# Pacing the first two tiles of an out-projection, and the queue order of one load and one cast

## The chip, the cores and the metric

The kernel runs on one NeuronCore of a Trainium2 chip. A core has engines that run side by side and meet only at semaphores: TensorE (PE) multiplies matrices, VectorE (DVE) and ScalarE (ACT) work element by element, GpSimd (POOL) does so more slowly, and SyncE (SP) mostly issues DMA transfers. Matmul results land in PSUM, eight banks per partition, from which DVE and ACT fetch them. The metric is the device time of one execution in microseconds (us), lower is better.

## What is computed

One layer of a hybrid decoder for 1024 positions of width 1024. After an RMS norm, one input projection gives the parts for eight heads of differential attention and four heads of gated linear attention (GLA). The attention part, which the change touches, is for each head

```python
s = einsum('bqhmd,bkhmd->bhmqk', qb, k)            # two maps m per head, q scaled
p = softmax(where(mask, s, -inf), axis=-1)         # causal
w = p[:, :, 0] - lam * p[:, :, 1]
o = einsum('bhqk,bhkv->bqhv', w, v)
...
oa = rms_norm(o, subln_g) * (1 - lam_init) * silu(ga)
y = einsum('bse,ed->bsd', concatenate([oa, ob], -1), w_out)   # out-projection, ob from GLA
out = x + rms_norm(y, post_g)
```

## The kernel before

**Precision and tiles.** Factors are split into a high and a low part (a rounding cast on ACT, then the remainder by a subtraction on DVE), and a product is three matmuls, high by high and the two mixed ones. The positions are eight tiles of 128; a matmul has up to 512 columns.

**Phase 1** (to about 624 us) projects the input and runs the GLA heads. It stores q, k, the values and the GLA output ("mix") to DRAM scratch, and at its end loads the first halves of the out-projection's weights (`wo_hi`, `wo_lo`, slices 8 to 15) and the first tile's mix (`mix0`).

**Phase 2** (to about 920 us) interleaves three streams of PE work, each a generator that yields the cost of what it just traced:

- `all_scores` (line 1223): for each head and each block of 128 queries, from the last (7) down to the first, and for both maps, the scores `sc` (two matmuls for each part of up to 512 keys, in one of three PSUM banks used in turn). DVE masks and reduces them to a minimum (`p<-sc,maskt`), ACT takes the exponential (`p<-p,stt`), POOL scales the second map's probabilities, and DVE subtracts them (`p<-p,stt,p`).
- `all_values` (line 1311): `turn` (1243) transposes these probabilities on PE (`wtr`), casts the high part on ACT (`wt_hi`, line 1253) and subtracts the low part on DVE (`wt_lo`). `weigh` (1257) multiplies them by the values (`po`), two turns behind. After the last one of a half, ACT copies the result to `o`, and `attn_norm` (1271) takes its norm: two squares on ACT (`fold`, line 1283, and `sq`), a sum on DVE, its high and low part (`sq_hl`), a matmul with ones (`ms`), and what follows from it (`r`, `gate`).
- `out_early` (line 1415): the out-projection of the GLA half (`ypart`), tile by tile in two PSUM banks, one for each half of the columns. In tile 0 a step is one slice for both halves, six matmuls, with a yield of 1.0 before and after it; in tiles 1 to 6 a step is three matmuls with a yield of 0.69. A finished bank is copied by ACT (`yst`) and stored. Later this stream does the attention half for heads that are done, and at the end, in `mix_pair` (1499), casts the last heads' mix (`m_hi<-m_raw`) and puts earlier sums into banks (`yps<-yp`) for the last products.

`merge` (line 1106) decides the order: each stream has a clock that runs from a begin to an end, a yield of cost c moves it by c times (end - begin) / total cost, and the stream whose clock is least traces next. The scores have 288 units of time for a cost of 8 x 20.3, from 0. The values begin at 32. `out_early` begins at -6 and ends at 342 with a total cost of 149.24, a number that is written out by hand. PE keeps the order so made (`keep_in_program_order` in `mm` and `tr`); so do the few DMAs marked in the same way. On ACT, DVE and POOL, and for the other DMAs of SP, the compiler sets the order, and each of these queues then runs in that order.

**What the change touches.** `mix(1)` (line 1422) loads the second tile's mix, two transfers of 512 KB issued by SP and kept in order; it is now called in the first step of `out_early`, after `v_first = load_v(0)` (line 1151) has issued head 0's values. `turn` writes the cast of `wt_hi` at line 1253; `attn_norm` its first square at 1283; `mix_pair` its cast at 1504.

After phase 2, `finish` (1592) ends the tiles one after the other: the last products, the norm of each row, and the output.

Of the kernel before, what the change touches and what calls it, by code (L numbers as in the profile page):

```python
# [10 lines left out]
AF = mybir.ActivationFunctionType  # L11
# [9 lines left out]
DA_HEADS = 8  # L21
# [10 lines left out]
def hymba_kernel(  # L32
# [42 lines left out]
    act, dve, pool = Queue(nc.scalar), Queue(nc.vector), Queue(nc.gpsimd)  # L75

    def fp(t):
        return t.bitcast(F32)

    def cols(half):  # L80
        return slice(half * 512, half * 512 + 512)
# [47 lines left out]
    def bank(i, shape, name):  # L129
        return psum.tile(shape, F32, tag=f"b{i}", name=name)  # L130
# [10 lines left out]
    def mm(*a, **k):  # L141
        tc.keep_in_program_order(pe.matmul(*a, **k))  # L142

    def tr(dst, src):
        tc.keep_in_program_order(pe.transpose(dst, src, ident))  # L145
# [114 lines left out]
    i = order.index((1, 4))  # L260
# [792 lines left out]
    E, wo = D // P, {}  # L1053
# [18 lines left out]
    def mix_tiles():  # L1072
        n_mix[0] += 1
        return [
            hw.tile([P, 8, P], F32R, tag=f"s2_{n}{n_mix[0] % 2}", name=f"m_{n}")
            for n in ("hi", "lo")
        ]

    def mix(st):

        part = mix_tiles()
        for t in range(2):
            ins = sp.dma_start(fp(part[t]), mixe[st, t])
            if st < 2:
                tc.keep_in_program_order(ins)
        return part
# [54 lines left out]
    def load_v(h):  # L1141
        v = [smp.tile([P, NT, P], F32R, tag="v", name=f"v{t}", bufs=4) for t in range(2)]
        for t in range(2):

            with tc.issue_after(qk_load[0]) if h else nullcontext():
                ins = sp.dma_start(fp(v[t]), v_d[h // 4][h % 4, t])
            if h == 0:
                tc.keep_in_program_order(ins)
        return v

    v_first = load_v(0)

    n_sc, n_tr = [0], [0]
# [5 lines left out]
    def tr_bank(name, shape):  # L1159
        n_tr[0] += 1  # L1160
        return bank(TR[n_tr[0] % 2], shape, name)
# [77 lines left out]
    def blocks_of(kt, half):  # L1239

        return range(max(kt - 4 * half, 0), 4)

    def turn(h, half, kts):

        pt = tr_bank("wtr", [P, 512])
        n = 0
        for kt in kts:
            for i in blocks_of(kt, half):
                tr(pt[:, n : n + P], w[h, 4 * half + i][:, kt * P : (kt + 1) * P])
                n += P  # L1250
        hi = smp.tile([P, 512], F32R, tag="wt_hi", name="wt_hi", bufs=3)
        lo = smp.tile([P, 512], F32R, tag="wt_lo", name="wt_lo", bufs=3)
        act.copy(hi[:, :n], pt[:, :n])
        dve.tensor_tensor(lo[:, :n], pt[:, :n], fp(hi[:, :n]), ALU.subtract)
        return hi, lo

# [14 lines left out]
    def attn_norm(h, half, o):  # L1271
        if h < DA_HEADS - 1:
            gate = smp.tile([P, 512], F32, tag="gate", name="gate", bufs=2)
        else:
            gate = kp.tile([P, 512], F32, tag=("q1", "k1")[half], name="gate")
        with tc.issue_after(qk_load[0]):
            sp.dma_start(gate, g_d[h][:, cols(half)])
        sq = smp.tile([P, 512], F32, tag="r", name="sq", bufs=1)


        hl = smp.tile([P, 512], F32R, tag="sq_hl", name="sq_hl", bufs=1)
        fold = smp.tile([P, 512], F32, tag="fold", name="fold", bufs=1)
        act.activation(fold[:64], o[64:], AF.Square)
        act.activation(sq[:64], o[:64], AF.Square)
        dve.tensor_tensor(sq[:64], sq[:64], fold[:64], ALU.add)
        act.copy(hl[:64], sq[:64])
        dve.tensor_tensor(hl[64:], sq[:64], fp(hl[:64]), ALU.subtract)
        if h == DA_HEADS - 1:

            dve.scalar_tensor_tensor(gate, o, sub_g, gate, ALU.mult, ALU.mult)  # L1290
        for _ in range(4):
            yield 0.0
        n_tr[0] += 1
        ms = bank(TR[n_tr[0] % 2], [P, 512], "ms")
        mm(ms, ones, hl, start=True, stop=True)
        if h == DA_HEADS - 1 and not half:
            opened[TR[n_tr[0] % 2]] = None
        r = smp.tile([P, 512], F32, tag="r", name="r", bufs=1)
        act.activation(r, ms, AF.Ln, bias=eps_t, scale=1.0 / P)
        act.activation(r, r, AF.Exp, scale=-0.5)  # L1300
        if h < DA_HEADS - 1:
            dve.scalar_tensor_tensor(r, o, sub_g, r, ALU.mult, ALU.mult)
            pool.tensor_tensor(gate, r, gate, ALU.mult)
            sp.dma_start(mixd[h * P : (h + 1) * P, cols(half)], gate)
            stored.append(h)
        else:
            dve.tensor_tensor(gate, gate, r, ALU.mult)
            last_mix[half] = gate
        yield 0.0
# [97 lines left out]
    def y_bank(st, dh, name):  # L1407
        return bank(Y[dh], [P, 512], name)
# [6 lines left out]
    def out_early():  # L1415

        part = mix0
        ps = [y_bank(0, dh, "ypart") for dh in range(2)]
        for e in range(E, E + 8):
            yield 1.0  # L1420
            if e == E:
                nxt = mix(1)
            for dh in range(2):
                times(ps[dh], part, E, dh, e, E + 7)
            yield 1.0
        for dh in range(2):
            sp.dma_start(yd[0][dh], y_tile(ps[dh]))
        for st in range(1, NT - 1):
            part, nxt = nxt, mix(st + 1)
            rows = slice(ENDS[st - 1] * P, ENDS[st - 1] * P + P)  # L1430
            sp.dma_start(out[0, rows, :], x[0, rows, :])
            for dh in range(2):
                ps = y_bank(st, dh, "ypart")
                for e in range(E, E + 8):
                    times(ps, part, E, dh, e, E + 7)
                    yield 0.69
                sp.dma_start(yd[st][dh], y_tile(ps))

        yield lambda: len(stored) >= 7
        part = nxt  # L1440
        ps = [y_bank(NT - 1, dh, "ypart") for dh in range(2)]
        raws_o = [load_mix(st, 0, 4) for st in ENDS[:3]]
        for e in range(E, E + 8):
            for dh in range(2):
                times(ps[dh], part, E, dh, e, E + 7)
                yield 0.69
            if e < E + 4:
                weights(e - E)
            if e == E + 6:
                nxt = mix_part(ENDS[0], 0, 4, raws_o.pop(0))  # L1450
        for dh in range(2):
            kept = sp.dma_start(yd[NT - 1][dh], y_tile(ps[dh]))
        for n, st in enumerate(ENDS):
            part = nxt
            if n == 1:
                yield lambda: len(stored) >= 8
            if n + 3 < NT:
                raws_o.append(load_mix(ENDS[n + 3], 0, 4))

            if 1 <= n <= 4:  # L1460
                with tc.issue_after(kept.ins), tc.issue_after(mix_load[0]):
                    weights(3 + n)
            if n + 1 < NT:
                nxt = mix_part(ENDS[n + 1], 0, 4, raws_o.pop(0))
            for dh in range(2):
                ps = y_bank(st, dh, "ypart")
                for e in range(4):
                    times(ps, part, 0, dh, e, 3)
                    yield 0.69
                pool.dma_start(yd[st][dh], y_tile(ps), accum_op=ALU.add)  # L1470
        yield lambda: len(stored) >= 2 * (DA_HEADS - 1) - 1
        mix_pair(0)
        for n, st in enumerate(ENDS[:2]):
            if n:
                yield lambda: scored
            for dh in range(2):
                seed(st, dh, (Y, SC)[n][dh], sums_of(n)[:, dh])
            yield 0.7
        for st in ENDS[:2]:
            for dh in range(2):  # L1480
                for e in range(4, 7):
                    last_times(st, dh, parts_d[st], e)
                    yield 0.69
            if st == ENDS[0]:
                mix_pair(2)
                seed(ENDS[2], 0, SC[2], sums_of(2)[:, 0])
# [12 lines left out]
    def mix_pair(n):  # L1499

        hi, lo = (t.rearrange("p (a b) c -> p a b c", b=4) for t in mix_tiles())
        for i, st in enumerate(ENDS[n : n + 2]):
            raw = load_mix(st, 4, 3)
            act.copy(hi[:, i, :3], raw[:, :3])
            dve.tensor_tensor(lo[:, i, :3], raw[:, :3], fp(hi[:, i, :3]), ALU.subtract)
            parts_d[st] = hi[:, i], lo[:, i]

# [174 lines left out]
```

## Time and profile before

| | |
|---|---|
| time, median of 3 runs | 972.58 us (972.37 to 972.94) |
| span of the profiled execution, first to last instruction | 971.1 us |
| granted TensorE clock, mean over the span | 0.999 |
| PE: matmuls, 620 to 640 us | 18.59 of 20 us busy |
| PE: matmuls, 640 to 660 us | 19.55 of 20 |
| PE: matmuls, 660 to 900 us | 239.97 of 240 |
| PE: matmuls, 900 to 920 us | 19.85 of 20 |
| PE: matmuls, 920 to 940 us | 19.57 of 20 |
| PE: matmuls, 940 to 960 us | 20.00 of 20 |

The time of a run is taken outside of the profile; the profiled execution has its span only, which lies 1.48 us under the median of the runs. A row of the order of time gives the start in us, the duration in us, the engine, the line, the operation, what it writes and reads, the shape, how many were merged, and in brackets how long the engine had been idle ahead of it and what ended that. A matmul's duration is longer than the time to the next one's start, since matmuls are pipelined: two that follow closely overlap in the record. A row of the waits gives the waiting engine and what it waited to do, the engine and result that it waited for, the sum in us, how often, and the longest. A row of the stages gives the stretch, its length, and then the busy time of PE, weight loads, DVE, ACT and POOL, each with its number of instructions, then the granted clock, the share of the DMA engines and GB/s.

### The profile page before, as it was taken

The numbers are of one execution on the slowest core, as the hardware profiler recorded it, in microseconds if no ns is written. First come the engines' busy times: TensorE is split into PE (matmuls) and PEld (weight loads), VectorE is DVE, ScalarE is ACT, GpSimd is POOL, SyncE is SP. The second block draws the span as 40 slices with busy tenths as digits, with TensorE's granted clock in tenths as the row PEclk, the third lists the DMA queues.
The fourth block names the chain that finished last, engine by engine and source line by source line (L and its number), as shares of the span: only waits on it lengthen the run. The fifth ranks groups of instructions, "written<-read, shape, count | busy, mean of one in ns | idle before, by whom it ended". The sixth has DMA issues, their size and how long they took to land.

```text
span 971.1 us, 15096 instructions
## 1 busy us (share of the span) xinstructions
PE 958.7 (99%) x4977; PEld 814.5 (84%) x4977; DVE 735.5 (76%) x1464; ACT 604.6 (62%) x1166; POOL 207.9 (21%) x266
## 2 busy tenths in 40 slices
PE   8999999999999999999999999999999999999997
PEld 7998988888888888888888888878888888888786
DVE  5996698897687686686766576587888888898554
ACT  8752364764667555576665344366786787887773
POOL 4300001212141221231100002121322222443322
PEclk9999999999999999999999999999999999999999
DMA  9433366578568987986754588996656769994777
GB/s 347 163 103 117 101 192 225 170 239 294 199 210 255 300 272 251 302 277 212 259 177 152 163 251 269 401 336 203 221 170 218 241 200 355 334 286 106 152 210 148
DMA packets 151293, 220.39 MB, mean 227 GB/s; under 512 B 15728, under 2 KB 86384, under 8 KB 151120
## 3 DMA queue, kind: packets, MB, share of 16 engines
q1 hardware_dynamic: 137056, 178.70, 56.8%
q0 software_dynamic: 14160, 40.74, 14.5%
q8 instruction: 39, 0.64, 0.3%
q14 instruction: 38, 0.31, 0.1%
HBM read 133.93 MB, written 88.60 MB: 229 GB/s over the span
## 4 chain that ended last, share of the span: by engine, by line
PE 94%; ACT 3%; DVE 1%; issue 1%; DMA 0%; POOL 0%; DVEq 0%; ACTq 0%; POOLq 0%
PE x L142 23%; PE z L142 16%; PE y L142 16%; PE ypart L142 13%; PE sc L142 7%; PE po L142 5%; PE yps L142 4%; PE wtr L145 3%; PE gpo L142 3%; PE kv L142 1%; ACT junk L66 1%; PE gkl_ps L142 1%; PE pa L142 1%; DVE p L66 1%; ACT h_hi L66 0%
## 5 line engine op out<-in xcount | busy, mean ns | idle before, releaser
L66 ACT CAST w<-w_raw 128x512 fp32r<-128x512 f32 (+1 forms) x150 | 98.0, 655 | 92.3 <-PE y L142 46.4
L66 DVE TENSOR_TENSOR w<-w_raw,w 128x512 fp32r<-128x512 f32 (+1 forms) x150 | 109.3, 732 | 48.8 <-ACT w L66 44.6
L66 ACT ACTIVATE p<-p,stt 128x896 f32<-128x896 f32 (+7 forms) x128 | 99.3, 777 | 36.2 <-DVE stt L66 35.2
L66 ACT COPY s<-x 128x512 f32<-128x512 f32 x82 | 47.8, 586 | 88.8 <-PE x L142 88.2
L66 POOL TENSOR_SCALAR p<-p,stt,lam 128x1024 f32<-128x1024 f32 (+3 forms) x64 | 56.2, 879 | 147.7 <-DVE stt L66 143.8
L66 DVE CUSTOM_DVE_ANT_0 p<-sc,maskt 128x512 f32<-128x512 f32 (+3 forms) x128 | 74.3, 585 | 14.2 <-PE sc L142 12.9
L66 POOL DMA_DIRECT2D wo_d<-wo_hi x32 | 17.5, 545 | 313.9 <-ACT wo_hi L66 313.9
L142 PE MATMUL z<-s_hi,w 128*128 128x512 f32 x320 | 80.2, 393 | 0.0
L142 PE MATMUL x<-s_hi,w 128*128 128x512 f32 x320 | 80.1, 392 | 0.0
L142 PE MATMUL y<-h_hi,w 128*128 128x512 f32 x320 | 80.0, 392 | 0.0
L142 PE MATMUL ypart<-wo_hi,m_hi 128*128 128x512 f32 x192 | 79.5, 414 | 0.1
L142 PE MATMUL ypart<-wo_hi,m_lo 128*128 128x512 f32 x192 | 75.5, 393 | 0.0
L142 PE MATMUL ypart<-wo_lo,m_hi 128*128 128x512 f32 x192 | 75.4, 393 | 0.0
L142 PE MATMUL sc<-k,q 128*128 128x512 f32 (+1 forms) x192 | 69.1, 363 | 1.4 <-DVE stt L66 1.3
L142 PEld LDWEIGHTS z<-s_hi,w 128*128 128x128 f32 x320 | 59.7, 188 | 12.3
L142 PEld LDWEIGHTS y<-h_hi,w 128*128 128x128 f32 x320 | 59.7, 188 | 12.3
L142 PEld LDWEIGHTS x<-s_hi,w 128*128 128x128 f32 x320 | 59.7, 188 | 12.3
L66 DVE TENSOR_TENSOR w_raw<-w_raw 128x512 f32<-128x512 f32 (+1 forms) x88 | 66.1, 751 | 1.9 <-DMA w_raw<-in_w_in_dram 0.8
L142 PE MATMUL sc<-ks,q 128*128 128x512 f32 (+1 forms) x192 | 66.0, 347 | 0.0
L66 ACT CAST wt_hi<-wtr 128x512 fp32r<-128x512 f32 (+1 forms) x80 | 42.8, 535 | 25.1 <-PE wtr L145 24.3
L66 DVE TENSOR_TENSOR wt_lo<-wtr,wt_hi 128x512 fp32r<-128x512 f32 (+1 forms) x80 | 50.6, 633 | 8.9 <-ACT wt_hi L66 8.2
L66 DVE TENSOR_TENSOR c<-z,s 128x512 f32<-128x512 f32 x48 | 32.8, 688 | 30.6 <-ACT s L66 20.3
(225 smaller groups left out, 2351.7 us busy)
## 6 DMA issues: line engine op xcount, KB each, us to landing
w_raw<-in_w_in_dram SPq DMA_DIRECT2D x48, 512.0 KB, 4.9
wo_d<-wo_hi POOLq DMA_DIRECT2D x32, 256.0 KB, 3.8
q<-q_d SPq DMA_DIRECT2D x32, 256.0 KB, 4.7
k<-k_d SPq DMA_DIRECT2D x32, 256.0 KB, 5.5
ks<-k_d SPq DMA_DIRECT2D x64, 128.0 KB, 6.0
v<-v_d SPq DMA_DIRECT2D x16, 512.0 KB, 7.0
wo_raw<-in_w_out_dram POOLq DMA_DIRECT2D x31, 256.0 KB, 4.8
wo_d<-gqd POOLq DMA_DIRECT2D x22, 256.0 KB, 4.2
```

What stands on the lines that cost most here:

```text
L66: ins = op(*a, **k)
L142: tc.keep_in_program_order(pe.matmul(*a, **k))
L145: tc.keep_in_program_order(pe.transpose(dst, src, ident))
```

## The change

There are three parts.

1. Pacing. In tile 0 the two yields of a step go from 1.0 to 0.8 each. In tile 1 the yield goes from 0.69 to 0.89. The total cost in the call of `merge` stays as it is.
2. Loading. `mix(1)` is called right after `merge` and its helpers are defined, just ahead of `load_v(0)`, so that SP issues the second tile's mix before the first head's values; tile 0's loop no longer calls it.
3. Casting. `turn` remembers its latest cast of `wt_hi`. For the last head, `attn_norm`'s first square, and for the second call of `mix_pair` its casts, are traced under `issue_after` of that cast: on ACT they stand behind it in the queue, with no semaphore.

```diff
+    mix1 = mix(1)
     v_first = load_v(0)
...
+    turned_last = []
+
     def turn(h, half, kts):
...
-        act.copy(hi[:, :n], pt[:, :n])
+        turned_last[:] = [act.copy(hi[:, :n], pt[:, :n]).ins]
...
-        act.activation(fold[:64], o[64:], AF.Square)
+        with tc.issue_after(turned_last[0]) if h == DA_HEADS - 1 else nullcontext():
+            act.activation(fold[:64], o[64:], AF.Square)
...
         for e in range(E, E + 8):
-            yield 1.0
-            if e == E:
-                nxt = mix(1)
+            yield 0.8
             for dh in range(2):
                 times(ps[dh], part, E, dh, e, E + 7)
-            yield 1.0
+            yield 0.8
+        nxt = mix1
...
-                    yield 0.69
+                    yield 0.89 if st == 1 else 0.69
...
             raw = load_mix(st, 4, 3)
-            act.copy(hi[:, i, :3], raw[:, :3])
+            with tc.issue_after(turned_last[0]) if n else nullcontext():
+                act.copy(hi[:, i, :3], raw[:, :3])
```

## The prediction

> **What bounds the kernel now.** I read the page first, then who waited for whom on TensorE (PE), then the order of time around each wait.
>
> ```profile
> span 971.1 us, 15096 instructions
> PE 958.7 (99%) x4977; PEld 814.5 (84%) x4977; DVE 735.5 (76%) x1464; ACT 604.6 (62%) x1166; POOL 207.9 (21%) x266
> PE 94%; ACT 3%; DVE 1%; issue 1%; DMA 0%; POOL 0%; DVEq 0%; ACTq 0%; POOLq 0%
> ```
>
> PE is busy for 958.7 of 971.1 us and is 94% of the chain that ended last. The change neither adds nor removes a matmul, so it can only win time in which PE waits. From 600 us to the end the waits view of PE has three rows:
>
> ```profile
> PE sc L142 <- DVE stt L66: 1.3, 2, 1.1
> PE po L142 <- ACT wt_hi L66: 0.5, 1, 0.5
> PE wtr L145 <- DVE p L66: 0.4, 1, 0.4
> ```
>
> Two waits of score matmuls for VectorE (DVE), one wait of an attention product for a ScalarE (ACT) cast, one of a transpose for DVE. But a matmul is recorded longer than its turn lasts, so part of a wait hides under "busy". I therefore measure between starts, in the order of time:
>
> ```profile
> 624.05 0.39 PE L142 MATMUL ypart<-wo_hi,m_hi 128*128 128x512 f32 x1
> ...
> 624.50 0.39 PE L142 MATMUL ypart<-wo_lo,m_hi 128*128 128x512 f32 x1
> 624.99 0.50 PE L142 MATMUL ypart<-wo_hi,m_hi 128*128 128x512 f32 x1
> ...
> 625.81 0.40 PE L142 MATMUL sc<-k,q 128*128 128x512 f32 x1
> ...
> 635.31 0.28 PE L142 MATMUL sc<-ks,q 128*128 128x256 f32 x1
> 635.81 0.50 PE L142 MATMUL sc<-k,q 128*128 128x512 f32 x1 [0.22 <-DVE stt L66]
> ...
> 638.64 0.28 PE L142 MATMUL sc<-ks,q 128*128 128x128 f32 x1
> 640.04 0.50 PE L142 MATMUL sc<-k,q 128*128 128x512 f32 x1 [1.12 <-DVE stt L66]
> ...
> 645.80 0.39 PE L142 MATMUL ypart<-wo_lo,m_hi 128*128 128x512 f32 x1
> 646.59 0.66 PE L145 MATMUL wtr<-ident,p 128*128 128x128 f32 x4 [0.40 <-DVE p L66]
> ```
>
> A matmul of 512 columns takes 0.228 us of PE (624.05 to 624.50 is two of them); narrower ones I scale by columns. So PE loses 0.49 - 0.23 = 0.26 us at 624.99, 0.50 - 0.11 = 0.39 at 635.81, 1.40 - 0.06 = 1.34 at 640.04 and 0.79 - 0.23 = 0.56 at 646.59. The first is a bank that phase 1 still holds; no edit touches it. The other three are 2.29 us, and they are what the pacing can win. The same reading at the end:
>
> ```profile
> 916.20 0.59 ACT L66 COPY o<-po 128x512 f32<-128x512 f32 x1 [0.85 <-PE po L142]
> ...
> 916.74 0.49 PE L145 MATMUL wtr<-ident,p 128*128 128x128 f32 x3
> 916.82 0.63 ACT L66 ACTIVATE fold<-o 64x512 f32<-64x512 f32 x1
> ...
> 918.48 0.91 ACT L66 CAST m_hi<-m_raw 128x384 fp32r<-128x384 f32 x2
> ...
> 919.29 0.58 ACT L66 COPY yps<-yp 128x512 f32<-128x512 f32 x1
> 919.45 0.40 PE L142 MATMUL yps<-wo_lo,m_hi 128*128 128x512 f32 x1
> 919.81 0.47 ACT L66 CAST wt_hi<-wtr 128x384 fp32r<-128x384 f32 x1
> ...
> 920.32 0.56 DVE L66 TENSOR_TENSOR wt_lo<-wtr,wt_hi 128x384 fp32r<-128x384 f32 x1
> 920.34 0.50 PE L142 MATMUL po<-wt_hi,v 128*128 128x256 f32 x2 [0.49 <-ACT wt_hi L66]
> ...
> 920.93 0.39 PE L142 MATMUL po<-wt_lo,v 128*128 128x256 f32 x1
> ...
> 921.35 0.69 DVE L66 TENSOR_TENSOR sq_hl<-sq,sq_hl 64x512 fp32r<-64x512 f32 x1 [0.48 <-ACT sq_hl L66]
> ...
> 922.18 0.41 PE L142 MATMUL ms<-sq_hl,ones 128*128 128x512 f32 x1
> ```
>
> The last transposes are done at 917.23 (916.74 + 0.49), but their cast starts at 919.81, behind fold, yst and sq (between the rows shown), two m_hi and a yps copy. PE waits 0.89 - 0.23 = 0.66 us for the high half and 0.59 - 0.23 = 0.36 for the low half: 1.02 us. After that PE runs to its last matmul without a wait worth naming, so what is won there comes off the end.
>
> **The pacing.** The planner gives the out-projection stream 348 units of time for 149.24 units of cost, 2.33 each. The first tile's step falls from 2.33 to 1.87, the second's grows from 1.61 to 2.08; 16 x 1.0 + 16 x 0.69 equals 16 x 0.8 + 16 x 0.89, so from the third tile on PE's order is the old one. By the merge rule the new order is: slices 8 and 9 ahead of the first score (now only 8), slices 8 to 14 ahead of the score (block 4, map 1) that waits at 640.04 (now 8 to 13), and, ahead of the first transpose (646.59), all of tile 0 and four half-slices of tile 1 (now one).
>
> So that score has 6 x 0.228 = 1.37 us more PE work ahead of it. That is not all won, since the first score too is 1.37 us later (627.18 for 625.81), and with it DVE's chain. But DVE has slack there:
>
> ```profile
> 628.31 0.75 DVE L66 CUSTOM_DVE_ANT_0 p<-sc,maskt,stt 128x512 f32<-128x512 f32 x1 [1.14 <-PE sc L142]
> ...
> 629.83 0.75 DVE L66 CUSTOM_DVE_ANT_0 p<-sc,maskt,stt 128x512 f32<-128x512 f32 x1
> ```
>
> It idles 1.14 us for the second score, because slice 9 stands between the first and the second. In the new order the scores 1 to 3 follow each other, slice 10 comes after them, and the fourth is through PE at about 627.18 + 3 x 0.46 + 1.37 + 0.6 = 630.55: its reduction moves from 629.83 to 630.55, by 0.7. The chain behind it (exponential, POOL's scaling, DVE's difference, next block) is paced by itself. PE is 1.37 later, the chain 0.7: **0.67 us** of the 1.73 at 635.81 and 640.04 goes, about 1.1 stays. Bounds: 0, if the chain slips as far as PE; 1.37, if it doesn't slip.
>
> ```profile
> 645.65 0.88 DVE L66 SCALAR_TENSOR_TENSOR p<-p,stt,p 128x640 f32<-128x640 f32 x1
> ...
> 651.41 0.63 PE L142 MATMUL po<-wt_hi,v 128*128 128x512 f32 x2
> ```
>
> The transpose at 646.59 waits for this DVE difference, which ended at 646.53. It gets 9 x 0.228 = 2.05 us more work ahead of it, less the 0.67, against a chain at most 0.7 later: **0.56 us** goes. Bounds: 0.2 and 0.56.
>
> What was pulled ahead is missing behind: from the transpose on, up to nine matmuls (2.05 us) less cover. I cost that at nothing, because DVE, which all waits there go back to, has gaps:
>
> ```profile
> 645.00:650.00 5.00, 4.60 (x30) 3.81 (x29) 4.70 (x18) 4.73 (x14) 2.00 (x3) 1.00 1.06 373
> 650.00:655.00 5.00, 5.00 (x27) 4.17 (x26) 4.55 (x15) 3.00 (x10) 1.06 (x3) 1.00 1.03 386
> 655.00:660.00 5.00, 5.00 (x26) 4.15 (x25) 3.10 (x8) 2.76 (x5) 1.21 (x1) 1.00 1.04 368
> ```
>
> DVE (third of the busy columns) is busy for 12.35 of these 15 us; the 2.65 idle cover the 2.05, but in 645 to 655 only 0.75 is free. If that cover fails, what was won early is paid back.
>
> **Mix ahead of values.** Tile 1 starts about 3 us earlier: now at 645.34 (the row at 645.80 is its third matmul), then 9 x 0.228 and the 0.67 sooner, some 642.6. Its mix is now issued behind the values:
>
> ```profile
> 634.39 1.08 SPq L1146 DMA_DIRECT2D v<-v_d  x2
> 635.51 0.43 SPq L1083 DMA_DIRECT2D m_hi<-mixe  x1
> 635.98 0.43 SPq L1083 DMA_DIRECT2D m_lo<-mixe  x1
> ...
> DMA to landing us min/median/max: 4.5/5.9/8.1
> ```
>
> With the two changed over it goes out at 634.4 and 634.9 (the store ahead of it in SP's queue stays), and at the median is there at 640.8, 1.8 us in time: **nothing**. At the longest, 8.1, it would be 643.0, 0.4 late; left behind the values it would land near 642 and have no margin. So the move is cover for the pacing, no gain of its own. The values lose 0.9 us; their first reader is the product at 651.41. The Trainium skill, "DMA: Bandwidth & Descriptors", section Specifications, gives 435 GB/s as the ceiling of the 16 engines; by that, an estimate, the 1 MB of the mix takes 2.4 us and there is no wait even at the worst place. The trace's times to landing are two to three times that, and I keep the 0 to 0.4.
>
> Tile 1 also needs the first tile's bank, which an ACT copy empties (0.59 us, as o's copy). Between the last matmul on that bank and the next one lie three matmuls and a narrow score, about 0.8 us, and the matmul itself ends 0.17 after its turn: 0 if ACT is free, one exponential if not:
>
> ```profile
> 640.08 0.94 ACT L66 ACTIVATE p<-p,stt 128x768 f32<-128x768 f32 x1 [1.45 <-DVE stt L66]
> ```
>
> I take 0, since ACT itself idled 1.45 us ahead of this one; 0.94 is the other end.
>
> **The cast first.** ACT's copy of o ends at 916.79 and the cast can start at 917.25; one or two of yst and sq, which the edit doesn't hold, fit ahead of it. Even at 918.5 the low half would be ready by 919.5, before 919.68, when PE wants it: 1.02 us goes. What is late next is the norm of half 1: fold now waits for the cast, so the sum of squares starts 0.5 to 1.0 us later, while PE reaches ms 1.02 earlier (921.16). The low half of sq_hl ends at 922.04 now; ACT has the same list to do, so I put it at about 921.35, and ms 0.15 later: 0.35 us of new wait. **0.67 us**; bounds 1.02 (no new wait) and -0.9 (below). The casts of m_hi are also held, but their readers come after 928.
>
> **Sum.** 0.67 + 0.56 + 0.67 = 1.9 us off 971.1: a span of 969.2. The runs' median, 972.58, is 1.48 above the profile's span, so **970.7**.
>
> **Rivals.**
> 1. All named waits go: the DVE chain doesn't slip and ms is in time. 1.73 + 0.56 + 1.02 = 3.31 us: 969.3. For it: DVE's 1.14 us gap. Against: the extra work ahead of the score is 1.37 us, so the last 0.36 needs another order on DVE. Chance 0.22.
> 2. The early wait only moves: with 0.75 us free on DVE in 645 to 655, the scores behind the transposes wait instead. Then only the end pays: 971.9. Chance 0.18.
> 3. The cast isn't moved, because the instruction remembered when fold is traced isn't the last one. By the order of the code (the last transposes are traced one step before fold) it is. Without the end's gain: 971.35. Chance 0.08.
> 4. Slower: ACT's queue is in order, and the compiler may set all that the edit doesn't hold (yst, sq, yps) ahead of the cast. From a cast at about 919.3 on, nothing is won at po, and fold starts at 920.2 for 916.82. Then fold 0.6, sum 0.7, cast 0.6, low half 0.7 and steps put ms at 923.0 or later instead of 922.18: +0.9, with two yps copies (1.1) between, +2.0. It makes the kernel slower only where the early part wins nothing as in 2: 973.5 to 974.6. Chance 0.08. The Trainium skill, "TensorE: Matmul & The Clock Gate", section Architectural detail, states that ScalarE and VectorE run strictly first in, first out; by that rule a cast that waits for PE also holds what stands behind it. The trace agrees: the cast was free at 917.23 and ran at 919.81.
>
> **How the numbers follow.** The forecast has 0.44, spread over 970.0 to 971.4. 0.2% (1.95 us, about what a measurement of this kernel can tell from no change) is 970.63, in the middle of that: half of it counts as faster, half as the same. Faster: 0.22 + 0.22 = 0.44. Same: 0.22 + 0.18 + 0.08 = 0.48. Slower: 0.08. The range from 969.2 to 972.7 leaves out the slower case and the lower half of the first rival, 0.19.
>
> **What would show it.** Right: the two score waits (0.22 and 1.12 in the rows) come to about 0.7; the transposes near 647 don't wait; tile 1 starts near 642.6 without a wait; wt_hi is cast before 918.6; po runs on and ms waits 0.3 or less; from 660 us on everything is some 1.2 us earlier, from 921 on 1.9. Wrong: a wait of sc between 648 and 660 as long as what was won; a wait of ypart for yst or for m_lo near 642; a wt_hi cast after 919.3; or new waits between 660 and 916, where the compiler's order on ACT and DVE may come out otherwise.

## The result and the profile after

The changed kernel takes 975.12 us (median of 12 runs, 973.28 to 978.8); the kernel before, run beside it, 973.01 (12 runs, 972.37 to 973.68). The ratio is 1.0026 [1.0015 to 1.0037] (a ratio here is estimated from all runs, so it can differ a little from the quotient of two medians): slower by 2.1 us between the medians, where 1.9 us faster was forecast, and outside of the forecast range. The runs of the changed kernel lie 5.5 us apart, those of the kernel before 1.3. The profiled execution of the changed kernel is its slowest run, 978.8; a second profile is read further down. One execution of hl_first, an experiment below, took 1189.71 us at a granted clock of 0.753 and is left out of its ratio.

The page after, its span and its busy times:

```profile
span 977.1 us, 15098 instructions
PE 961.9 (98%) x4977; PEld 816.3 (84%) x4977; DVE 735.9 (75%) x1464; ACT 605.3 (62%) x1166; POOL 205.6 (21%) x266
```

The span has grown by 6.0 us, and PE's busy time by 3.2 with the same number of matmuls: so there are 2.8 us more of waiting, and matmuls that take longer. The waits of PE from 590 us on, after:

```profile
PE sc L142 <- DMA ks<-k_d: 1.9, 1, 1.9
PE sc L142 <- DMA k<-k_d: 1.1, 1, 1.1
PE ms L142 <- DVE sq_hl L66: 1.1, 1, 1.1
PE sc L142 <- DVE stt L66: 0.5, 2, 0.3
PE sc L142 <- DMA q<-q_d: 0.2, 1, 0.2
```

The waits for `wt_hi` and for `p` are gone, and that for DVE has shrunk from 1.3 to 0.5. New are three waits of scores for the loads of q, k and ks, which PE did not wait for before, and one of `ms`. The order of time of PE, after, around these places:

```profile
638.89 0.39 PE L142 MATMUL ypart<-wo_lo,m_hi 128*128 128x512 f32 x1
639.57 0.50 PE L142 MATMUL sc<-k,q 128*128 128x512 f32 x1 [0.29 <-DVE stt L66]
...
640.35 0.27 PE L142 MATMUL sc<-ks,q 128*128 128x128 f32 x1
640.82 0.50 PE L142 MATMUL sc<-k,q 128*128 128x512 f32 x1 [0.20 <-DVE stt L66]
...
642.94 0.49 PE L142 MATMUL ypart<-wo_hi,m_hi 128*128 128x512 f32 x1
...
647.16 0.39 PE L142 MATMUL ypart<-wo_lo,m_hi 128*128 128x512 f32 x1
647.67 0.66 PE L145 MATMUL wtr<-ident,p 128*128 128x128 f32 x4
...
650.87 0.62 PE L145 MATMUL wtr<-ident,p 128*128 128x128 f32 x4
651.68 0.47 PE L142 MATMUL sc<-k,q 128*128 128x512 f32 x1 [0.19 <-DMA q<-q_d]
...
653.36 0.39 PE L142 MATMUL po<-wt_lo,v 128*128 128x512 f32 x1
654.88 0.47 PE L142 MATMUL sc<-k,q 128*128 128x512 f32 x1 [1.14 <-DMA k<-k_d]
657.27 0.80 PE L142 MATMUL sc<-ks,q 128*128 128x512 f32 x1 [1.91 <-DMA ks<-k_d]
657.86 0.63 PE L142 MATMUL sc<-k,q 128*128 128x512 f32 x1
```

Measured between starts, less 0.228 us for 512 columns, as in the prediction: the two score waits are 0.45 + 0.41 = 0.86 us where they were 1.73, and the wait of the transpose 0.28 where it was 0.56. That is 1.15 us won by 648 us. Then PE loses 0.43 us for q (0.58, less 0.15 that stood after a transpose before too), 1.29 for k and 2.16 for ks: 3.9 us. And from 657.27 on a full matmul takes 0.43 us (657.86 to the next start at 658.29) in place of 0.228. The stages of after show why; the granted clock is the third value from the end:

```profile
650.00:657.00 7.00, 4.03 (x20) 2.77 (x18) 4.23 (x15) 2.87 (x10) 1.22 (x2) 0.97 1.06 290
657.00:663.00 6.00, 5.73 (x16) 4.56 (x17) 2.86 (x9) 2.40 (x5) 0.45 (x1) 0.50 1.03 346
```

In the six microseconds behind the long waits PE is granted half its clock (narrower stages put the half clock from 656.58, inside the last wait, to 663.40), and in the 6.14 us from 657.27 to 663.41 it does 3.2 us of work: another 2.9 us lost. Won 1.15, lost 3.9 and 2.9 is 5.6 us later; the same attention product starts at 917.77 us before and at 923.54 after, 5.77 later. So nearly all of the 6.0 us arises between 650 and 664 us, in a stretch to which the prediction gave no cost at all.

Why the loads are late is to be seen in SP's queue. Before, the order of its issues (start, duration of the issue, what is moved):

```profile
642.33 0.92 SPq L1031 DMA_DIRECT2D q<-q_d  x2
...
644.13 2.37 SPq L1034 DMA_DIRECT2D ks<-k_d  x4
646.60 1.00 SPq L1427 DMA_DIRECT2D y_d<-yst  x2
647.73 0.40 SPq L1083 DMA_DIRECT2D m_hi<-mixe  x1
```

And after:

```profile
642.74 0.33 SPq L1083 DMA_DIRECT2D m_lo<-mixe  x1
643.80 0.33 SPq L1430 DMA_DIRECT2D y_d<-yst  x1
644.99 0.32 SPq L1083 DMA_DIRECT2D m_hi<-mixe  x1
645.85 0.32 SPq L1031 DMA_DIRECT2D q<-q_d  x1
646.66 0.32 SPq L1430 DMA_DIRECT2D y_d<-yst  x1
647.18 0.32 SPq L1031 DMA_DIRECT2D q<-q_d  x1
647.58 1.00 SPq L1031 DMA_DIRECT2D k<-k_d  x2
649.05 2.96 SPq L1034 DMA_DIRECT2D ks<-k_d  x4
```

Before, the second half of the next head's loads (q, k and ks for keys 512 to 1023 of head 1) goes out at 642.3 to 646.5, ahead of tile 0's two stores (`y_d<-yst`, 256 KB each) and tile 2's mix (two transfers of 512 KB). After, the stores and the mix stand ahead: `m_lo` at 642.74, the first store at 643.80, `m_hi` at 644.99, the second store at 646.66, and ks starts at 649.05 instead of 644.13, 4.9 us later. SP itself waits on the way; two of the waits of SP's queue between 632 and 656 us, after, both ahead of `m_lo` at 642.74:

```profile
SPq L1083 <- DMA v<-v_d: 1.6, 1, 1.6
SPq L1083 <- PE ypart L142: 1.1, 1, 1.1
```

The first is a wait until an earlier transfer has landed; the other rows of that view, all but one of them of this kind, have no single wait above 0.9 us, and among them the issues of ks wait 0.7 us for `m_hi` and 0.5 for `m_lo`. The second is another thing: tile 2's mix goes into a buffer that PE's products of tile 0 still read, and so it holds SP for 1.1 us. The chain of work that ended last, after, goes through the store and the load:

```profile
643.80 5.90 DMA y_d<-yst
...
649.71 7.51 DMA ks<-k_d
```

A store that the pacing has made early lands at 649.70; by this chain a ks load follows it, and PE waits for that load. Both kernels keep all 16 DMA engines busy there (from 640 to 650 us their share is 1.03 before and 1.04 after, from 650 to 657 it is 1.03 and 1.06), so a transfer that is set ahead takes its time from those behind it.

### The profile page after: what moved, and what is told of

It is laid out like the page before. It is cut to its first block, busy times and chain, and to the rows that moved or that the text cites. A ratio compares the mean times of both kernels' runs of the same rounds, so it can differ in the third digit from the quotient of the medians.

```text
span 977.1 us, 15098 instructions
## 1 busy us (share of the span) xinstructions
PE 961.9 (98%) x4977; PEld 816.3 (84%) x4977; DVE 735.9 (75%) x1464; ACT 605.3 (62%) x1166; POOL 205.6 (21%) x266
## 4 chain that ended last, share of the span: by engine, by line
PE 93%; DMA 2%; ACT 2%; DVE 1%; issue 1%; SPq 0%; POOL 0%; DVEq 0%; ACTq 0%; POOLq 0%
PE x L142 23%; PE z L142 16%; PE y L142 16%; PE ypart L142 13%; PE sc L142 7%; PE po L142 5%; PE yps L142 4%; PE wtr L145 3%; PE gpo L142 3%; PE kv L142 1%; DMA w_raw<-in_w_in_dram 1%; DMA ks<-k_d 1%; PE gkl_ps L142 1%; PE pa L142 1%; DMA y_d<-yst 1%
```

## The experiments

**Theory A.** The loss comes from the order of SP's queue. Tile 0's stores and tile 2's mix are traced by the out-projection stream when tile 0 is through. With steps of 0.8 that is at clock -6 + 2.332 x 12.8 = 23.85 of the planner, with steps of 1.0 at -6 + 2.332 x 16 = 31.3. Head 1's second loads are traced by the score stream at clock 25.0 in both. So the pacing has set 1.5 MB ahead of them. **Rival B** is the second rival of the prediction: the matmuls pulled ahead are missing as cover, and PE would stand there whatever SP does. **Theory C** is on the end: the cast won its 1.02 us at `po` and hands it on to `ms`.

**loads_behind.** The kernel before, with nothing changed but the order of the loads: head 1's loads of this place in the code are traced later, and its second half is held behind tile 2's mix (`mix2` is the last transfer of that mix).

```diff
-                if qb == 4 and h + 1 < DA_HEADS:
+                if qb == (4 if h else 2) and h + 1 < DA_HEADS:
                     for n in ("q", "k", "ks"):
-                        load_qk(h + 1, n, 1)
+                        with nullcontext() if h else tc.issue_after(mix2[0]):
+                            load_qk(h + 1, n, 1)
```

> The kernel before, with PE's order as it was; only on SP's queue are head 1's loads of q, k and ks for keys 512 to 1023 put behind tile 0's two stores and tile 2's mix, where the changed kernel has them. Theory A (the loss is the queue: these loads go out some 4 us later, and head 1's first scores wait for them): PE waits of sc for k or ks by DMA, together 2 to 4 us, between 650 and 660 us, and 2 to 6 us more than before, with a wide scatter. Theory B (the loss is the pacing: the second tile's thinner fill lets PE wait): no such wait, and the time of before within 0.5 us.

Measured: 976.68 us (5 runs) beside 973.27 for the kernel before, ratio 1.0033 [1.0020 to 1.0046]. Two of its waits of PE are new:

```profile
PE sc L142 <- DMA ks<-k_d: 1.3, 1, 1.3
PE sc L142 <- DMA q<-q_d: 1.0, 1, 1.0
```

Between starts they are 1.44 (0.15 of it stood there before) and 1.55 us, together 2.8 of the 3.4 by which the median is higher. The pacing, the mix and the cast are as before in this kernel; the order in SP's queue by itself makes the loss. The clock stays at 1.00.

**loads_first.** The changed kernel, with tile 0's stores and tile 2's mix put back behind head 1's loads (the bank is still copied out at once, into `kept0`; `head1` is the last of head 1's loads):

```diff
-        for dh in range(2):
-            sp.dma_start(yd[0][dh], y_tile(ps[dh]))
+        kept0 = [y_tile(ps[dh]) for dh in range(2)]
         for st in range(1, NT - 1):
-            part, nxt = nxt, mix(st + 1)
+            part, nxt = nxt, mix(st + 1) if st > 1 else None
...
+                    if (st, dh, e) == (1, 0, E + 3):
+                        with tc.issue_after(head1[0]):
+                            for i in range(2):
+                                sp.dma_start(yd[0][i], kept0[i])
+                            nxt = mix(2)
```

> The changed kernel, with tile 0's two stores and tile 2's mix held on SP's queue until head 1's loads have been issued; PE's order is that of the change. Theory A: no wait of sc for a DMA; the score waits come to about 0.9 us as in the changed kernel (1.7 before) and the transpose wait to about 0.3 (0.6), the end costs about 0.2 more than before: 0.6 to 1.1 us faster than before. Theory B: the lost time stays between 647 and 665 us under another name, and the kernel is 1 to 4 us slower than before.

Measured: 972.33 us (11 runs), ratio to the kernel before 0.9991 [0.9982 to 1.0]. SP's queue has the old order again:

```profile
646.07 2.37 SPq L1034 DMA_DIRECT2D ks<-k_d  x4
648.53 1.00 SPq L1443 DMA_DIRECT2D y_d<-yst  x2
```

and these are all the waits of PE from 590 us on:

```profile
PE ms L142 <- DVE sq_hl L66: 1.1, 1, 1.1
PE sc L142 <- DVE stt L66: 0.5, 2, 0.3
```

The pacing is in this kernel in full, the cover behind is as thin as in the changed one, and nothing waits between 648 and 916 us. A stands, B falls. The early gain (0.89 us at the scores, 0.30 at the transpose) arrives all but 0.2 us: the last transposes start at 915.73 us instead of 916.74, 1.01 earlier.

**pacing_alone.** The kernel before with the yields of part 1 (0.8 and 0.89) alone.

```diff
-            yield 1.0
+            yield 0.8
...
-                    yield 0.69
+                    yield 0.89 if st == 1 else 0.69
```

> The kernel before with the new pacing alone; the second tile's mix stays behind the values and the casts as they were. Its queue on SP has head 1's loads behind tile 0's stores and tile 2's mix, as in the changed kernel. Theory A: sc waits for DMAs of q, k or ks between 650 and 660 us, 2 to 4 us in all, and 1 to 5 us more than before; the end as before. Theory B gives the same time here, but with a wait for DVE or ACT in that place.

Measured: 975.88 us (7 runs, 972.64 to 977.34) beside 973.0, ratio 1.0023 [1.0010 to 1.0036]: the whole loss of the change comes from this part. Its profile has one wait for a load, `sc` for ks, 1.65 us between starts, less than was expected; that run took 974.59, 1.3 below the median. How long the loads are late differs from run to run.

**mix_alone.** The kernel before with part 2, the mix of tile 1 ahead of the values.

```diff
+    mix1 = mix(1)
     v_first = load_v(0)
...
-            if e == E:
-                nxt = mix(1)
```

> The kernel before with the second tile's mix loaded ahead of head 0's values, nothing else; the orders on PE, DVE, ACT and POOL are those of before. Every theory: within 0.5 us of before, no new wait of PE.

Measured: 972.83 us (11 runs), ratio 0.9998 [0.9989 to 1.0007], no new wait. It costs and brings nothing.

**cast_alone.** The kernel before with part 3, the cast.

```diff
+        with tc.issue_after(turned_last[0]) if h == DA_HEADS - 1 else nullcontext():
+            act.activation(fold[:64], o[64:], AF.Square)
...
+            with tc.issue_after(turned_last[0]) if n else nullcontext():
+                act.copy(hi[:, i, :3], raw[:, :3])
```

> The kernel before, with the cast part alone: the last turned weights ahead of the last head's first square and of the second mix pair. Theory C (the wait only moves from po to ms, since the cast of sq_hl now stands behind the mix casts and the copies on ACT): no wait of po, a wait of ms for sq_hl of about 1.1 us, and 0 to 0.4 us slower than before. The prediction's reading: ms waits 0.35 us and the kernel is 0.5 to 0.8 us faster. Neither has a wait near 650 us.

Measured: 973.12 us (11 runs), ratio 1.0000 [0.9991 to 1.0009]. The wait of `po` is gone, and in its place stands the wait of `ms`, 1.23 us between starts. C holds: the cast by itself is worth nothing. But two casts of `m_hi` and two copies of `yps` stood ahead of the cast of `sq_hl` in the kernel before too:

```profile
920.71 0.62 ACT L66 CAST sq_hl<-sq 64x512 fp32r<-64x512 f32 x1
```

That is 4.51 us after the start of the copy `o` at 916.20. In cast_alone the same nine pieces of work precede it in another order, and it starts 4.71 us after that copy (917.21 to 921.92): 0.2 us later, and not earlier, so what PE no longer waits at `po` it waits at `ms`.

**loads_first_no_cast.** The kernel before with the pacing, and the stores and tile 2's mix held as in loads_first; neither the mix of tile 1 nor the cast is moved.

```diff
-            yield 1.0
+            yield 0.8
...
-                    yield 0.69
+                    yield 0.89 if st == 1 else 0.69
...
+                        with tc.issue_after(head1[0]):
+                            for i in range(2):
+                                sp.dma_start(yd[0][i], kept0[i])
+                            nxt = mix(2)
```

> Pacing alone, without the cast part and with the second tile's mix behind the values as before; tile 0's stores and tile 2's mix are held behind head 1's loads. Theory A: no wait of sc for a DMA; the early part gains about 1.1 us and the end is that of before: 0.8 to 1.4 us faster than before. If the mix had to go ahead of the values, ypart waits for m_lo near 642 us, 0.3 to 1 us. Theory B: 1 to 4 us slower than before.

Measured: 972.67 us (11 runs), ratio 0.9991 [0.9982 to 1.0]. The median gain of 0.6 us is below what was expected; the ratio makes it 0.9, and its interval takes in the whole expected range. `ypart` doesn't wait for tile 1's mix, which is issued behind the values here: moving it wasn't needed for this pacing.

**after_again.** The changed kernel, unaltered, profiled a second time: no profile of the other kernels at the full clock has six microseconds at half of it.

```diff
 (no edit)
```

> The changed kernel once more, for a second profile. Theory A: sc waits for DMAs of q, k or ks between 650 and 660 us, 1.5 to 4 us in all, and the time follows that sum; where PE's waits are shorter than in the first profile, the granted clock stays at 1.00 from 640 to 680 us and the time is 973.5 to 975.5; where they are as long, the clock drops to about 0.9 there, and the time is 977 or more.

Measured: 977.38 us, granted clock 0.999. Its waits for loads, from the waits of PE:

```profile
PE sc L142 <- DMA q<-q_d: 2.2, 2, 1.5
PE sc L142 <- DMA k<-k_d: 1.2, 1, 1.2
```

The first row holds two waits: 0.66 us of a score for q, and 1.53 of the score that reads ks, which the view puts down to q as well. Between starts, with 0.15 taken off the first as above, they are 0.90, 1.40 and 1.77 us, 4.1 in all, no shorter than the 3.9 of the first profile. Yet the clock stays at 1.00. So the waits come back and the half clock doesn't: the expectation that an equal sum of waits lowers the clock was wrong. The longest single wait was shorter, though, 1.77 us for 2.16.

**hl_first.** loads_first, and on ACT the casts of `m_hi` and the `yps` copies of `mix_pair`'s second call held behind the cast of `sq_hl`, for which `ms` waits. What was ahead of that cast, in the order of time of the changed kernel:

```profile
923.65 0.47 ACT L66 CAST wt_hi<-wtr 128x384 fp32r<-128x384 f32 x1
...
924.80 0.93 ACT L66 CAST m_hi<-m_raw 128x384 fp32r<-128x384 f32 x2
...
924.88 0.69 DVE L66 TENSOR_TENSOR sq<-sq,fold 64x512 f32<-64x512 f32 x1 [0.17 <-ACT fold L66]
...
925.63 1.10 ACT L66 COPY yps<-yp 128x512 f32<-128x512 f32 x2
...
926.67 0.61 ACT L66 CAST sq_hl<-sq 64x512 fp32r<-64x512 f32 x1
```

The sum was there at 925.57, its cast started 1.10 us later, behind two `m_hi` and two `yps`.

```diff
-        act.copy(hl[:64], sq[:64])
+        hl_cast[h, half] = act.copy(hl[:64], sq[:64]).ins
...
-            with tc.issue_after(turned_last[0]) if n else nullcontext():
+            with tc.issue_after(hl_cast[DA_HEADS - 1, 1]) if n else nullcontext():
                 act.copy(hi[:, i, :3], raw[:, :3])
...
+            with tc.issue_after(hl_cast[DA_HEADS - 1, 1]) if n else nullcontext():
                 for dh in range(2):
                     seed(st, dh, (Y, SC)[n][dh], sums_of(n)[:, dh])
```

> The changed kernel with head 1's loads ahead of tile 0's stores and tile 2's mix, as in the run with the loads first, and with the mix casts of the second pair and the seeds of the second tile held on ACT behind the cast of sq_hl, no longer behind that of wt_hi. Theory C (ms waits because that cast stands behind mix casts and copies): the wait of ms falls from 1.23 us between starts to 0.2 to 0.6, po still doesn't wait; 0.6 to 1.0 us faster than with the loads first, 1.5 to 2.0 faster than before. If the norm's chain itself is the limit, ms still waits 1 us and nothing is gained.

**hl_first_again.** The same kernel, run and profiled once more.

> The same kernel as in the run with sq_hl first, for a profile at the full clock. If theory C holds, ms waits 0.2 to 0.6 us (1.23 with the loads first) and something later takes the gain back: a new wait of PE between 922 us and the end, or a longer tail after its last matmul. If ms still waits 1 us, the norm's own chain is the limit.

Measured: ratios 0.9994 [0.9985 to 1.0003] both times, 972.42 us in the second (10 runs): no gain over loads_first, where 0.6 to 1.0 us was expected. Its profile shows where it went. The wait of `ms` is gone (0.16 us between starts), and two others have come:

```profile
PE yps L142 <- ACT m_hi L66: 0.3, 1, 0.3
PE yps L142 <- DVE m_lo L66: 0.2, 1, 0.2
```

Between starts they are 0.50 + 0.51 us at 925.6 and 926.4: the last products wait for the gate of the last norm, whose first step on ACT (`r`) now stands behind the casts and copies that were moved.

**fold_free.** hl_first, with `fold` no longer held behind the last `wt_hi`; the cast of `sq_hl` is held in its place.

```diff
-        with tc.issue_after(turned_last[0]) if h == DA_HEADS - 1 else nullcontext():
-            act.activation(fold[:64], o[64:], AF.Square)
+        act.activation(fold[:64], o[64:], AF.Square)
...
-        hl_cast[h, half] = act.copy(hl[:64], sq[:64]).ins
+        with tc.issue_after(turned_last[0]) if h == DA_HEADS - 1 else nullcontext():
+            hl_cast[h, half] = act.copy(hl[:64], sq[:64]).ins
```

> As with sq_hl first, but the first square of the last head isn't held behind the cast of wt_hi; the cast of sq_hl is. On ACT the order is o, fold, yst, sq, wt_hi, a copy, sq_hl, then the mix casts. Theory C: both waits are nearly gone, po 0 to 0.3 us and ms 0 to 0.4 between starts, and the kernel is 0.8 to 1.2 us faster than with the loads first, 1.7 to 2.1 faster than before. If the end is set by something else than PE's order, it is within 0.3 us of the run with the loads first.

Measured: 972.06 us (11 runs), ratio 0.9989 [0.9980 to 0.9998]. Neither `po` nor `ms` waits; `m_hi` and `m_lo` still cost 0.31 + 0.51. The gain over loads_first is some 0.3 us between the medians, a third of what was expected, and the two intervals overlap.

**r_first.** fold_free, with one more `yps` copy held behind the norm's `r`.

```diff
-        act.activation(r, r, AF.Exp, scale=-0.5)
+        norm_ln[h, half] = act.activation(r, r, AF.Exp, scale=-0.5).ins
...
-                seed(ENDS[2], 0, SC[2], sums_of(2)[:, 0])
+                with tc.issue_after(norm_ln[DA_HEADS - 1, 1]):
+                    seed(ENDS[2], 0, SC[2], sums_of(2)[:, 0])
```

> As with the fold free, and the seed of the third tile's first half (a copy yps<-yp on ACT) held behind the exponential of the last norm's first half. Theory D (after po and ms, PE now waits for the last mix's cast m_hi<-gate because the norm's logarithm stands behind copies and casts on ACT; the queue of ACT between 916 and 926 us is the bound, and each reorder hands the wait on): the two waits for m_hi and m_lo, 0.31 and 0.51 us, shrink by 0.3 to 0.6 in all, and a wait for the held seed of 0 to 0.6 us appears; the time is within 0.6 us of the run with the fold free. If ACT's order isn't the limit, the waits for m_hi and m_lo stay as they are.

Measured: 971.79 us (11 runs, 971.41 to 972.53) beside 972.89 for the kernel before, ratio 0.9989 [0.9980 to 0.9998]: the lowest median of all, 1.1 us below the kernel before. The ratio is that of fold_free, so the last step by itself isn't shown to win anything. `m_hi` and `m_lo` don't wait any more, and instead

```profile
PE yps L142 <- ACT yps L66: 0.6, 1, 0.6
```

0.71 us between starts, for the very copy that was held. **Theory D**, formed on the way: at the end ACT's queue is the bound. The rows of ACT in the order of time of r_first, between the cast that `ms` waits for and the norm's `r`:

```profile
918.80 0.62 ACT L66 CAST sq_hl<-sq 64x512 fp32r<-64x512 f32 x1
919.32 1.11 ACT L66 COPY yps<-yp 128x512 f32<-128x512 f32 x2
920.36 0.93 ACT L66 CAST m_hi<-m_raw 128x384 fp32r<-128x384 f32 x2
921.19 0.58 ACT L66 COPY o<-po 128x512 f32<-128x512 f32 x1
921.67 0.69 ACT L66 ACTIVATE r<-ms,eps_t 128x512 f32<-128x512 f32 x1
```

None has an idle time ahead of it, so an order which frees one reader may keep another waiting. The sums of what PE loses there, kernel by kernel: 1.02 us before (`po`), 1.23 in loads_first (`ms`), 1.01 in hl_first_again (`m_hi`, `m_lo`), 0.82 in fold_free, 0.71 in r_first. By these sums reordering has won 0.3 us of about 1. The test that would settle D, less work on ACT in this stretch, wasn't run.

## Why the prediction was wrong

- **What bounds the kernel, and what can be won:** right. The three early waits and the one of `po` are what the change could reach.
- **The score waits:** right, forecast 0.67 of 1.73 us, measured 0.87. The DVE chain slips there as was worked out: the fourth reduction starts at 630.57 us (forecast 630.55).
- **The transpose:** forecast all of 0.56, measured 0.28, inside its bounds of 0.2 and 0.56. The DVE difference that it waits for ended at 647.61 for 646.53, 1.08 us later and not at most 0.7, so the transpose still starts right behind it. The two terms together come to 1.15 us for 1.23.
- **The cover missing behind, costed at nothing:** right. loads_first has no wait between 648 and 916 us, with the cover just as thin. The second rival's mechanism falls.
- **Mix ahead of values, costed at nothing, and the bank's copy at 0:** right. Tile 1 starts at 642.94 us without a wait (forecast 642.6), and mix_alone is at 0.9998. It was no cover for the pacing either: without it `ypart` doesn't wait.
- **The pacing's DMAs: this step failed.** "From the third tile on PE's order is the old one" was true, and the prediction stopped at PE. Tile 0's end is a step that issues DMAs too: two stores and, by `mix(st + 1)`, tile 2's mix. It moved from 31.3 to 23.85 on the planner's clock, past the score stream's loads at 25.0. SP's queue is in order and the DMA engines there were full (the stages before gave 1.06 and 1.03), so the loads that PE needs next went out 4.9 us later. The sum had no term for this. Of the signs named under "wrong", a wait of `sc` between 648 and 660 was the right place, with another cause. loads_behind makes the loss without the pacing, loads_first takes it away with the pacing in: that is shown. The Trainium skill, "DMA: Bandwidth & Descriptors", section Anatomy of one DMA — SWDGE (gpsimd) path, states that an issue waits for its semaphores on the issuing sequencer, not in a DMA engine. The trace after agrees: SP itself waited 1.1 us for a `ypart` of tile 0 before it issued `m_lo`, and all that stood behind it in SP's queue waited too.
- **The cast: a term mis-sized.** The first half is right: 1.02 us goes at `po`, and `wt_hi` is cast at 923.65, which less the 5.77 us of delay is 917.9 (forecast before 918.6). The second half was mis-sized: the new wait of `ms` was put at 0.35 us and measured 1.23, so that the term is -0.2 and not +0.67. The prediction says that ACT has the same list to do, and yet lets the low half of `sq_hl` end 0.69 us earlier, at 921.35 for 922.04. The list was the same, and the low half ended at 928.00, which less the delay is 922.23: 0.19 later. PE's 1.02 and these 0.19 make the wait. `m_hi` and `yps`, whose readers come late, stand ahead of the cast of `sq_hl`, whose reader is early. The fourth rival named ACT's order as the danger, with `wt_hi` as the one kept back; it was `sq_hl`.
- **The sum:** 1.15 - 0.2 would have been 0.95 us faster, and that is about what loads_first measures (973.27 - 972.33 = 0.94; between the profiles' spans, 971.1 and 970.3, it is 0.8). Half of the forecast gain was never there; the rest, and 2.1 us more, went to the loads.

The half clock costs 2.9 us in the first profile and nothing in the second. Its part in the median is small: 6.8 us at half a clock lower the mean over the span by 0.0035, and of the 12 runs the profiled one had a mean granted clock of 0.995, two had 0.997, and the other nine 0.998 or 0.999, as the runs of the kernel before. So most of what the change loses is the waits.

## What to carry to other kernels

When a step of a planned stream is moved, list every DMA that it issues, and ask past which loads it moves in the issuing queue; PE's order alone doesn't show it, and the price falls on another stream. A gain and a loss can be told apart with one kernel that reproduces the loss without the gain and one that keeps the gain without the loss. Where an engine has no idle time, as ACT between 918.8 and 922.4 us in r_first, ask of each operation put first who reads what now stands behind it.

## What was not expected of the hardware

The half clock: in the first profile of the changed kernel PE stood for 1.29 us, ran one matmul, stood for 2.16 us, and was granted 0.50 from 656.58 to 663.40. The second profile had gaps of 1.40 and 1.77 us at the same places and no drop, loads_behind 1.44 and 1.55, also none. The Trainium skill, "TensorE: Matmul & The Clock Gate", Part 1, states that the clock is halved after an idle window of about 3.4 us that runs freely, and comes back after about as long a busy one. The 0.50 agrees; each gap here is shorter than that window, and if the window had to be idle from end to end no drop was to be looked for.

The traces show more. The half clock lasted 6.83 us, twice 3.41. Behind PE's last matmul the clock drops once more, at 974.02 us, 317.44 us after the first drop, which is 93 times 3.413: the drops lie on one grid. Counted back from the drops at the end (974.02, 973.09 and 973.72 us), the grid has a window of the first profile from 653.16 to 656.58 us, with the first gap and most of the second in it: PE was busy for 1.06 of these 3.41 us, and the drop is at the window's end. In the second profile a border at 655.65 parts the gaps, and PE was busy for 2.12 and 1.88 us of the windows beside it; in loads_behind, for 2.38 and 2.10. So two gaps that fall in one window can halve the clock, where about the same waiting, parted by a border, doesn't. That is an account of three profiles after the fact; no run moved the gaps against the grid to test it.

The scatter: two of the three kernels in which PE waits for loads vary more than the rest. The changed kernel's runs span 5.5 us and pacing_alone's 4.7, loads_first's 1.2 and r_first's 1.1, though the five of loads_behind only 1.8. The same score's wait for ks is seen at another length in each profile (idle 1.91 us, then 1.53, then 1.48 in pacing_alone and 1.31 in loads_behind), so one profile of such a kernel is one draw.
